# Expert products as plain 4-byte products in four column groups of 32, without splitting their operands

## The chip, the cores and the metric

The kernel runs on one core of a Trainium2 chip. The metric is the device time of one execution in microseconds. Before the change three runs gave a median of 1053.33 us (1052.43 to 1054.62).

## The reference

A two-branch encoder block over 512 tokens (and 16 learned ones ahead of them) with 1024 features, followed by a layer of 16 experts. What is changed lies in the experts. All tensors are 4-byte floats.

```python
h = layer_norm(DN_ALPHA * h + mixed, ln1_g, ln1_b)
ffn = moe_ffn(h, w_router, w_gate, w_up, w_down)
h = layer_norm(DN_ALPHA * h + ffn, ln2_g, ln2_b)
...
def moe_ffn(x, ...):
    # each token goes to the two best experts of its best group of four
    for e in range(N_EXPERTS):                       # 16
        h = silu(t @ w_gate[e]) * (t @ w_up[e])      # 1024 -> 512
        out = out + comb[:, e:e + 1] * (h @ w_down[e])   # 512 -> 1024
```

## The kernel before, in words

The span has three parts. Up to about 655 us the two branches of the mixer run; the change leaves them alone. From 655 to 729 us come the output projection, the first post-LN and the router. From 729 us on the 16 experts run, and behind them the second post-LN with the stores.

**The experts.** `order` (line 902) lets the four groups take turns, so that four experts in a row have no token in common. Each expert works only on its own tokens. Their places in a list of at most `CAP` = 112 come from the router (`idx`, one column for each expert), and their weights from `wsl`. For each expert:

- `gather` (line 1151) is an indirect DMA on GpSimd's queue that brings the tokens' rows from `h_dram` into `xg`.
- `xprep` (line 1159) transposes them by eight TensorE transposes with `ident` (L1164). ScalarE copies the result rounded (`xh`), VectorE subtracts for the rest (`xl`).
- `gu` (line 1168) makes the gate or the up product, 8 steps of 128 features into one PSUM tile `gu` of 128 places x 512 columns.
- `act` and `htr` (line 1195) multiply `silu(gate)` with up into `sg` and transpose it in four pieces (L1199), again split in `hh` and `hl`.
- `down` (line 1202) makes the down product into `py`, 4 steps of 128 x 2 halves of 512 columns.
- `add_rows` (line 1233) scales the rows by the tokens' weights on ScalarE and adds them to `o_dram` by one indirect DMA on GpSimd's queue, `scatter` (line 1155).

**The split.** No product takes 4-byte floats as they are. `split` and `unit` (line 1120) make from each megabyte of weights a rounded half `wh` (a cast on ScalarE, L233) and a lower half `wl` (a subtraction on VectorE, L236). One product then is three TensorE products, x-high with w-high, x-high with w-low, x-low with w-high. That gives 24 for gate, 24 for up and 24 for down, each 512 columns wide.

**Weights.** An expert has 6 MB, in six DMAs of 1 MB that SyncE issues (`fetch`, line 1109, which has the line 1114 in the waits). `slot` (line 1101) takes the next of 16 buffers in turn; SyncE waits until the split has read what was there.

**Order.** Every engine executes its instructions in the order in which a scheduler put them. In the loop at the end of the file the order of the program is: gate of expert i, `htr` of expert i-1, up of expert i, `xprep` of expert i+1, down of expert i-1. The scheduler interleaves them where operands come later. `overflow` counts experts that have more than `CAP` tokens; for the inputs here there is none, so that the loop for them at the end runs zero times. The first expert's tokens don't come by a gather. `place` (line 1043) picks them by products from the tiles `v` (`pso<-xg,v` in the profile). Line 91 is that of a helper that records instructions in program order; many rows have it.

The last expert runs beside the one before it and the second post-LN (`finish`, line 1288): its down product goes into two tiles `pye`, and the rows of `o_dram` are loaded back for the post-LN.

Of the kernel before, what the change touches and what calls it, by code (L numbers as in the profile page):

```python
# [22 lines left out]
S = 512  # L23
# [20 lines left out]
NX = 9  # L44
CAP = 112
# [3 lines left out]
RZ = 3  # L49
RMW = 240  # L50
FX = 1
H3, L3 = 1, 0
S3 = 2
S4 = 1
# [24 lines left out]
# the bits of the first guess of -1 / sqrt(2 x) are SEED less half those of x  # L79
# [3 lines left out]
class InOrder:  # L83
    """an engine whose instructions keep the order of the program"""
# [10 lines left out]
def hybrid_kernel(ctx, tc, x, meta_tokens, ln_in_g, ln_in_b, w_router, w_in, conv_w, conv_b,  # L95
# [27 lines left out]
    # ---------------------------------------------------------------- constants  # L123
# [31 lines left out]
    G.memset(epsc, EPS2)  # L155
    idx = consts.tile([128, NE], I32, name="idx")
    wsl = consts.tile([128, NE], F32, name="wsl")
    rest = consts.tile([128, NT], I32, name="rest")
# [57 lines left out]

    def halves(shape):
        """a pair for a split; while there is a third buffer it takes its turn"""
# [19 lines left out]
    # ---------------------------------------------------------------- phase 1  # L238
    with ExitStack() as p1:
# [14 lines left out]
        # as wide as the room between this pool and the next, so that the last scratch tiles make way for a slot  # L254
# [97 lines left out]
        # ---- head: input LayerNorm, transposes, split  # L352
# [52 lines left out]
        # mean and 1 / sqrt(var + eps) of two tiles and the meta tokens, then of the other two tiles  # L405
# [20 lines left out]
        # the weights of dt: four copies of the heads over the partitions  # L426
# [66 lines left out]
        # the residual in token layout waits in DRAM for the first post-LN  # L493
# [12 lines left out]
        # ---- dt and the cumulative decay  # L506
# [54 lines left out]
        # ---- pooling branch and gates  # L561
# [58 lines left out]
        # the router: scaled by the first post-LN, its column sums and its product with that LN's  # L620
        # shift, the latter two on every partition
# [13 lines left out]
        # ---- SSD: chunks of 128 tokens after one of the 16 meta tokens  # L635
# [120 lines left out]
        def g_out(g, wgt=None, ts=range(NT), ps2=()):  # L756
# [3 lines left out]
            for t, hf in [(t, hf) for t in ts for hf in range(2)]:  # L760
# [10 lines left out]
                if (t, hf) in POOLED.get(g, ()):  # L771
                    # the last groups' convolutions leave scratch tiles behind
# [136 lines left out]
        with tc.high_priority():  # L909
            G_ = InOrder(tc, G)  # L910
            for t in range(NT):
                (Q if t < QV else G_).dma_start(vt[t], h_dram[t * 128:(t + 1) * 128, :])
                if t == FX:
                    G_.dma_start(first, wu[order[0], 512:].rearrange("(k p) c -> p k c", p=128))
# [205 lines left out]
    def unit(r):  # L1120
        """a megabyte of expert weights, split in two"""
        ns[0] += 1
        if ns[0] <= 4:
            wh, wl = halves(r.shape)
            if ns[0] == 2:
                nsp[0] = 0
# [437 lines left out]
```

## Time and profile before

| | before |
|---|---|
| median of three runs | 1053.33 us |
| profiled execution, its span | 1047.7 us |
| TensorE (PE) busy in the span | 974.9 us |
| VectorE (DVE) busy | 805.0 us |
| ScalarE (ACT) busy | 520.1 us |
| GpSimd (POOL) busy | 189.1 us |
| first expert product starts at | 728.96 us |
| last product of the last `up` starts at | 1009.95 us |

The span is from the first to the last instruction of the profiled execution; the runs' time holds 5.6 us more. A row of the timeline has the start of the first instruction of a group in us from the span's start, the time until the end of the last, the engine, the line, the operation, the result and operands by name and shape, and the count. Consecutive instructions of one kind are drawn together. TensorE's ends are modelled, and its instructions overlap, so the distance from one start to the next tells what one costs. `PEld` is TensorE's loading of the stationary operand. In square brackets stands how long the engine was idle before, and what released it.

### The profile page before, as it was taken

The numbers are of one execution on the slowest core, as the hardware profiler recorded it, in microseconds if no ns is written. First come the engines' busy times: TensorE is split into PE (matmuls) and PEld (weight loads), VectorE is DVE, ScalarE is ACT, GpSimd is POOL, SyncE is SP. The second block draws the span as 40 slices with busy tenths as digits, with TensorE's granted clock in tenths as the row PEclk, the third lists the DMA queues.
The fourth block names the chain that finished last, engine by engine and source line by source line (L and its number), as shares of the span: only waits on it lengthen the run. The fifth ranks groups of instructions, "written<-read, shape, count | busy, mean of one in ns | idle before, by whom it ended". The sixth has DMA issues, their size and how long they took to land. (4 is left out here: it accounts for less than half of the span.)

```text
span 1047.7 us, 14476 instructions
## 1 busy us (share of the span) xinstructions
PE 974.9 (93%) x5664; PEld 842.5 (80%) x5664; DVE 805.0 (77%) x1225; ACT 520.1 (50%) x551; POOL 189.1 (18%) x129
## 2 busy tenths in 40 slices
PE   4989999999999999999999879989999999999970
PEld 3878888999898998989899767768788888888860
DVE  6887652476868686969797888398999999998973
ACT  4434333433525242525244352134778787888863
POOL 4930000000000000000000264144222222212134
PEclk9989999999999999999999998998999999999995
DMA  7442455423233232314232343975999999999854
GB/s 221 133 161 98 133 158 155 148 84 103 80 96 121 86 131 87 130 56 152 70 121 101 136 163 127 400 280 181 307 356 356 357 343 356 333 339 365 318 153 81
DMA packets 111350, 198.41 MB, mean 189 GB/s; under 512 B 7866, under 2 KB 54306, under 8 KB 110256
## 3 DMA queue, kind: packets, MB, share of 16 engines
q1 hardware_dynamic: 98320, 163.24, 45.6%
q0 software_dynamic: 6816, 18.09, 6.4%
q10 hardware_dynamic: 6144, 16.13, 4.2%
q8 instruction: 45, 0.74, 0.3%
q14 instruction: 25, 0.20, 0.1%
HBM read 186.05 MB, written 20.05 MB: 197 GB/s over the span
## 5 line engine op out<-in xcount | busy, mean ns | idle before, releaser
L236 DVE TENSOR_TENSOR wl<-raw,wh 128x2048 fp32r<-128x2048 f32 (+1 forms) x145 | 295.6, 2056 | 71.6 <-ACT wh L233 59.9
L233 ACT CAST wh<-raw 128x2048 fp32r<-128x2048 f32 (+1 forms) x145 | 242.8, 1696 | 164.3 <-PE ss L767 64.0
L1180 PE MATMUL gu<-wh,xhl 128*128 128x512 f32 x496 | 154.0, 394 | 0.1
L277 PE MATMUL mm<-hH,wh 128*128 128x264 f32 x624 | 129.1, 288 | 5.8 <-ACT ze L569 5.1
L277 PE MATMUL mm<-hH,wl 128*128 128x264 f32 x624 | 128.2, 287 | 0.0
L277 PE MATMUL mm<-hL,wh 128*128 128x264 f32 x624 | 127.7, 286 | 0.0
L776 POOL TENSOR_TENSOR acc<-acc,pre 128x512 f32<-128x512 f32 x12 | 19.2, 1621 | 529.2 <-ACT pre L775 529.2
L277 PEld LDWEIGHTS mm<-hH,wh 128*128 128x128 f32 x624 | 99.4, 190 | 9.1 <-ACT ze L569 5.3
L1180 PEld LDWEIGHTS gu<-wh,xhl 128*128 128x128 f32 x496 | 91.9, 188 | 18.3 <-DVE xhl L1166 0.5
L295 PE MATMUL mm<-hH,wh 128*128 128x512 f32 x256 | 102.5, 400 | 0.0
L295 PE MATMUL mm<-hL,wh 128*128 128x512 f32 x256 | 101.6, 397 | 0.0
L295 PE MATMUL mm<-hH,wl 128*128 128x512 f32 x256 | 101.5, 397 | 0.0
L277 PEld LDWEIGHTS mm<-hH,wl 128*128 128x128 f32 x624 | 98.4, 190 | 1.1
L277 PEld LDWEIGHTS mm<-hL,wh 128*128 128x128 f32 x624 | 97.7, 190 | 0.2
L1180 PE MATMUL gu<-wl,xhl 128*128 128x512 f32 x248 | 96.5, 394 | 0.0
L767 PE MATMUL ss<-wh,yy 128*128 128x512 f32 x192 | 67.4, 410 | 0.0
L1217 PE MATMUL py<-wh,hhl 128*128 128x512 f32 x224 | 67.0, 390 | 0.0
L295 PEld LDWEIGHTS mm<-hH,wl 128*128 128x128 f32 x256 | 48.2, 188 | 10.4
L295 PEld LDWEIGHTS mm<-hH,wh 128*128 128x128 f32 x256 | 48.2, 188 | 10.2
L295 PEld LDWEIGHTS mm<-hL,wh 128*128 128x128 f32 x256 | 48.1, 188 | 10.3
L1180 PEld LDWEIGHTS gu<-wl,xhl 128*128 128x128 f32 x248 | 46.5, 188 | 9.9
L1157 POOL DMA_INDIRECT o_dram<-hb,idx x13 | 26.0, 2000 | 153.4 <-ACT hb L1236 153.2
(373 smaller groups left out, 1752.9 us busy)
## 6 DMA issues: line engine op xcount, KB each, us to landing
raw<-in_w_exp_up_dram SPq DMA_DIRECT2D x29, 1024.0 KB, 14.4
raw<-in_w_exp_down_dram SPq DMA_DIRECT2D x29, 1024.0 KB, 14.8
raw<-in_w_in_dram SPq DMA_DIRECT2D x28, 1024.0 KB, 6.2
raw<-in_w_exp_gate_dram SPq DMA_DIRECT2D x28, 1024.0 KB, 17.0
M<-aD ACTq DMA_DIRECT2D x8, 1024.0 KB, 4.7
raw<-in_w_in_dram SPq DMA_DIRECT2D x16, 512.0 KB, 5.0
raw<-in_w_ssd_out_dram SPq DMA_DIRECT2D x8, 1024.0 KB, 4.9
ze<-eD ACTq DMA_DIRECT2D x16, 256.0 KB
```

The costliest lines, as they stand in the source:

```text
L233: A.copy(wh[:, c], src[:, c])
L236: (E[i] if E else V).tensor_sub(wl[:, c], src[:, c], wh[:, c])
L277: T.matmul(ps[:, i, :HF], lhsT=w[:, k, cs], rhs=h[k][:, i * HF:(i + 1) * HF], start=(n == 0), stop=(n == 3 * KT - 1))
L295: T.matmul(ps, lhsT=w[:, k, cs], rhs=h[k][:, NM:], start=(n == 0), stop=(n == 3 * KT - 1))
L767: T.matmul(ps, lhsT=y[:, j, t * 128:(t + 1) * 128], rhs=w[:, j, hf * 512:(hf + 1) * 512], start=(n == 0), stop=(n == 5))
L776: G.tensor_add(a, a, f)
L1157: return G.indirect_dma_start(out=dst, out_offset=off(ix), in_=src[:n], in_offset=None, **lim, **kw)
L1180: T.matmul(ps, lhsT=(xh, xh, xl)[n][:, u, k, :], rhs=us[u][n == 1][:, k, :], start=(i == 0), stop=(i == len(ms) - 1))
L1217: T.matmul(py[hf], lhsT=x_[:, 2 * u + k, :], rhs=ww[:, k, hf * 512:(hf + 1) * 512], start=(u == 0 and k == 0 and n == 0), stop=(u == 1 and ...
```

## The change

An expert's gate, up and down products take the 4-byte operands as they are, without a split. Only the last expert's down product stays as it was. A product has a stationary operand of 32 places instead of 128, and four such products, whose results go to different quarters of the PSUM partitions, are issued one after the other (`quad`). The room for places shrinks from 112 to 96 = 3 x 32. The first 64 places take half of the columns in each of the four groups: in a step of `gu` four products of 256 columns, two blocks of places by two halves. The last 32 places take a quarter of the columns in each: four products of 128. For `down` these are 512 and 256 columns.

The layout that comes out has consequences. `silu`, the multiplication and the copies are 384 wide instead of 512. `htr` has three transposes instead of four. A row of the result holds half of a token's columns or a quarter, so that `add_rows` adds by two scatters with tables of their own (`ixq`, `wq`, made by two small products at line 1103 from `sel`). Gate and up weights are fetched with pairs of neighbouring rows on a partition (`rows2`, 4 KB in one piece instead of 2), and the tokens are transposed with every second column (`cols2`). The buffers of the splits join the weight buffers, which are now 22.

```diff
-NX = 9
-CAP = 112
+NX = 10
+CAP = 96
+BK = 32
...
+    def rows2(E, r, src, r0):
+        n = r.shape[1] * 128
+        E.dma_start(r.rearrange("p (q j) c -> p q (j c)", j=2),
+                    src[r0:r0 + n, :].rearrange("(q p j) c -> p q (j c)", p=128, j=2))
...
-        us0 = [split(wg_[0], 4, copies=1)]
...
+        iws = small("iws", 2 * NE)
+        V.tensor_copy(iws, iw)
...
+        for i in range(2):
+            sel = xg1[:, 512 + 128 * i:640 + 128 * i]
+            T.matmul(pq[:, 2 * NE * i:2 * NE * (i + 1)], lhsT=sel, rhs=iws, start=True, stop=True)
...
-            A.copy(xh[:, i], p)
-            V.tensor_sub(xl[:, i], p, xh[:, i])
+            if i:
+                V.tensor_copy(xT[:, 4:, :n], p[:, :, :n])
+            else:
+                A.copy(xT[:, :4, :n], p[:, :, :n])
...
+    def quad(p, lhs, rhs, m, **kw):
+        for j in range(4):
+            T.matmul(p[BK * j:BK * (j + 1), m], lhsT=lhs(j), rhs=rhs(j), **kw)
...
     def gu(src, ws=None):
-        ms = [(u, k, n) for u in range(2) for k in range(4) for n in (0, 2, 1)]
-            T.matmul(ps, lhsT=(xh, xh, xl)[n][:, u, k, :], rhs=us[u][n == 1][:, k, :],
-                     start=(i == 0), stop=(i == len(ms) - 1))
+        for n in range(KT):
+            w, k = ws[n // 4], n % 4
+            quad(ps, lambda j: xT[:, n, BK * (j // 2):BK * (j // 2) + BK],
+                 lambda j: w[:, k, 256 * (j % 2):256 * (j % 2) + 256], slice(0, 256), start=(n == 0), stop=False)
+            quad(ps, lambda j: xT[:, n, 2 * BK:3 * BK], lambda j: w[:, k, 128 * j:128 * j + 128],
+                 slice(256, 384), start=False, stop=(n == KT - 1))
...
     def down(src, ws=None):
+        for n in range(4):
+            u, k = n // 2, n % 2
+            w = ws[u]
+            quad(p[:, 0], lambda j: hT[:, k, 2 * BK * (j // 2) + BK * u:2 * BK * (j // 2) + BK * u + BK],
+                 lambda j: w[:, k, 512 * (j % 2):512 * (j % 2) + 512], slice(0, 512), start=(n == 0), stop=(n == 3))
+            quad(p[:, 1], lambda j: hT[:, 2, BK * n:BK * n + BK], lambda j: w[:, k, 256 * j:256 * j + 256],
+                 slice(0, 256), start=(n == 0), stop=(n == 3))
...
-        A.activation(ys, py[2], AF.Copy, scale=w_)
-        sc = scatter(o_dram[:, :], fl(ys), ix, compute_op=OP.add).ins
+        for q, (c, n) in enumerate(((slice(0, 512), 2), (slice(512, 768), 4))):
+            A.activation(ys[:, c], p[:, q, :1024 // n], AF.Copy, scale=col_of(wq[q], i))
+            sc = scatter(o_dram[:, :].rearrange("s (h c) -> (s h) c", h=n), ys[:, c], col_of(ixq[q], i),
+                         compute_op=OP.add).ins
```

On TensorE, in the middle of the experts, the program before goes from the down products of one expert over both kinds of transposes to the up products of the next, and interleaves down and up. A row has the line, the operation, the result and operands, the result's partitions x columns and the waits; `wh` and `wl` are the halves of the weights, `xhl` and `hhl` those of the tokens.

```order
L1217 MATMUL py<-wl,hhl 128x512 x2
L1217 MATMUL py<-wh,hhl 128x512 x2
L1217 MATMUL py<-wh,hhl 128x512 [waits Activation_49]
L1199 MATMUL pt<-ident,sg 128x128 [waits DVE_49]
L1199 MATMUL pt<-ident,sg 128x128 x3
L1164 MATMUL pt<-ident,xg 128x128 [waits DMASW4_49]
L1164 MATMUL pt<-ident,xg 128x128 x3
L1180 MATMUL gu<-wh,xhl 128x512 [waits Activation_49]
L1180 MATMUL gu<-wh,xhl 128x512
L1217 MATMUL py<-wl,hhl 128x512 [waits DVE_49]
```

Each product there is a third of a step, and the transposes stand among them. The program after has at the same place, on TensorE, whole blocks; `raw` is a weight buffer as fetched, and `xT` and `hT` are the transposed tokens and hidden rows.

```order
L1181 MATMUL gu<-raw,xT 32x256 x4
L1181 MATMUL gu<-raw,xT 32x128 x4
L1172 MATMUL pt<-ident,xg_5731 128x96 [waits DMASW1_49,PE_49]
L1172 MATMUL pt<-ident,xg_5731 128x96 x3
L1172 MATMUL pt<-ident,xg_5731 128x96 [waits PE_49]
L1172 MATMUL pt<-ident,xg_5731 128x96 x3
L1181 MATMUL py<-raw,hT 32x512 [waits DMAHW5_49,Activation_49]
L1181 MATMUL py<-raw,hT 32x512 x3
L1181 MATMUL py<-raw,hT 32x256 x4
```

`xprep` now stands ahead of a whole `down`, and between quads; the three `htr` transposes stand in the same way between a gate and an up product. The waits for the lower halves are gone, and those for the fetches (DMAHW) stand at the products themselves.

At the start of the experts TensorE has, before, the first gate products behind the last small products of the router.

```order
L91 MATMUL ss<-to_6322,R 128x32 [waits DVE_49,Activation_49]
L91 MATMUL ss<-to_6329,R 128x32 [waits DVE_49,Activation_49]
L1180 MATMUL gu<-wh,xhl 128x512 [waits Activation_49]
L1180 MATMUL gu<-wh,xhl 128x512 x3
L1180 MATMUL gu<-wl,xhl 128x512 x4
```

After, the count for `overflow` (`py<-ohs,onesb`, which stood between the gate products) and the two products for the scatter tables stand between the router's last products and the first quad.

```order
L1447 LDWEIGHTS onesb
L1447 MATMUL py<-ohs,onesb 128x16
L1103 MATMUL ss<-iws,xg_5731 128x32 [waits DVE_49] x2
L1181 MATMUL gu<-rawh,xT 32x256 [waits DMAHW7_49]
L1181 MATMUL gu<-rawh,xT 32x256 x3
L1181 MATMUL gu<-rawh,xT 32x128 x4
```

The wait of the `ss<-iws` products is for VectorE's copy of the tokens' places and weights to `iws`, and the first quad stands behind it.

## Rows read from the trace of the kernel before

**Rows 1.** The page, section 1: busy us (share) and instructions of each engine.

```profile
PE 974.9 (93%) x5664; PEld 842.5 (80%) x5664; DVE 805.0 (77%) x1225; ACT 520.1 (50%) x551; POOL 189.1 (18%) x129
```

**Rows 2.** Windows: PE, PEld, DVE, ACT, POOL busy us (count), clock, DMA share, GB/s.

```profile
800.00:850.00 50.00, 50.00 (x239) 41.48 (x239) 45.57 (x32) 41.90 (x35) 13.23 (x6) 1.00 1.03 355
```

**Rows 3.** Waits of SyncE's queue from 700 to 1010 us: us in total, times, longest.

```profile
SPq L1114 <- DVE wl L236: 121.8, 46, 7.8
```

**Rows 4.** Timeline of PE around the start of the experts.

```profile
716.08 1.95 PE L91 MATMUL pso<-xg,v 128*128 128x128 f32 x16
...
728.59 0.53 PE L91 MATMUL ss<-to,R 128*128 128x32 f32 x4
728.96 1.17 PE L1180 MATMUL gu<-wh,xhl 128*128 128x512 f32 x4
...
737.36 1.06 PE L1164 MATMUL pt<-ident,xg 128*128 128x128 f32 x8 [2.46 <-DMA xg<-h_dram,idx]
```

**Rows 5.** Timeline of PE over one expert, from one group of htr transposes to the next.

```profile
759.37 0.60 PE L1199 MATMUL pt<-ident,sg 128*128 128x128 f32 x4
...
763.23 0.39 PE L1180 MATMUL gu<-wl,xhl 128*128 128x512 f32 x1
763.46 0.61 PE L1180 MATMUL gu<-wh,xhl 128*128 128x512 f32 x2
763.91 0.39 PE L1180 MATMUL gu<-wl,xhl 128*128 128x512 f32 x1
...
777.12 0.60 PE L1199 MATMUL pt<-ident,sg 128*128 128x128 f32 x4
777.56 0.60 PE L1164 MATMUL pt<-ident,xg 128*128 128x128 f32 x4
```

**Rows 6.** Timeline of the end: last up product, transposes, last down product, loads of o_dram.

```profile
1009.95 0.39 PE L91 MATMUL gu<-wl,xhl 128*128 128x512 f32 x1
...
1011.12 0.66 PE L91 MATMUL pt<-ident,sg 128*128 128x128 f32 x4 [0.78 <-DVE sg L91]
...
1012.45 0.73 PE L91 MATMUL pye<-wh,hhl 128*128 128x512 f32 x2 [0.68 <-ACT hhl L91]
1012.51 1.98 SPq L91 DMA_DIRECT2D raw<-o_dram  x4
```

**Rows 7.** Groups by form, PE, whole span: count, busy us, mean ns, idle before.

```profile
L722 PE MATMUL ss<-bc,XP 128*128 128x128 f32 x128 | 18.0, 281 | 0.0
L726 PE MATMUL ss<-M,XP 128*64 128x128 f32 x256 | 17.5, 279 | 0.0
...
L705 PE MATMUL ss<-Xd,Bk 128*128 128x256 f32 x32 | 9.3, 378 | 0.0
```

**Rows 8.** Timeline of PE in the mixer: whole-width products (L722) and two column groups (L726).

```profile
307.62 1.05 PE L722 MATMUL ss<-bc,XP 128*128 128x128 f32 x8
308.61 1.09 PE L726 MATMUL ss<-M,XP 128*64 128x128 f32 x16
309.63 1.16 PE L722 MATMUL ss<-bc,XP 128*128 128x128 f32 x8
310.72 1.09 PE L726 MATMUL ss<-M,XP 128*64 128x128 f32 x16
```

**Rows 9.** Timeline of PE: 256 columns (L705), 128x1 (L749) and small 2-byte products (L1388).

```profile
283.16 0.59 PE L705 MATMUL ss<-Xd,Bk 128*128 128x256 f32 x2
...
329.59 0.95 PE L749 MATMUL ss<-ones,ze 128*128 128x1 f32 x8
...
733.62 0.26 PE L1388 MATMUL py<-ohs,onesb 128*128 128x16 bf16 x4
```

**Rows 10.** Timeline of DVE in the router: pieces of a weight split.

```profile
708.17 2.50 DVE L236 TENSOR_TENSOR wl<-rawh,wh 128x512 fp32r<-128x512 f32 x4 [0.31 <-ACT wh L235]
```

**Rows 11.** Timeline of POOL in the experts: a scatter and a gather.

```profile
765.09 1.90 POOL L1157 DMA_INDIRECT o_dram<-hb,idx  x1 [10.78 <-ACT hb L1236]
767.30 2.52 POOL L1153 DMA_INDIRECT xg<-h_dram,idx  x1 [0.30 <-issue]
```

More of the change, by code (lines that the diff above doesn't have):

```diff
@@ new lines, in tile_of @@
+    def tile_of(pool, tag, **kw):
+        return lambda shape, dt: pool.tile(list(shape), dt, name="raw", tag=tag, **kw)
+    one, two = dict(bufs=1), dict(bufs=2)
+    places = ([tile_of(wsp, "wl3", **one)] + [tile_of(rawp, "raw")] * RP
+              + [tile_of(rawx[i], "raw") for i in range(RX - 2, -1, -1)]
+              + [hb_(1)] + [tile_of(ga, t) for t in ("ze", "XP", "yHL", "M")]
+              + [tile_of(wsp, t, **two) for t in ("wh", "wl")] * 2 + [tile_of(rawz, "raw")] * RZ
+              + [tile_of(hpool, "hL0"), tile_of(wsp, "wh3", **one), hb_(0), tile_of(rawx[RX - 1], "raw")])
@@ L1115, in fetch @@
             rs.append(r)
         return rs
-    ns = [1]
[L1120 to L1126, printed above, removed]
-            n = r.shape[1] // (0, 1, S3, S4)[ns[0] - 1]
-            for c in (slice(i, i + n) for i in range(0, r.shape[1], n)):
-                with tc.issue_after(exs[-1]):
-                    A.copy(wh[:, c], r[:, c])
-                with tc.issue_after(x_ins[-1]):
-                    V.tensor_sub(wl[:, c], r[:, c], wh[:, c])
-            return wh, wl
-        return split(r, 2 if ns[0] % 6 in SPL else 1)
@@ L1199, in htr @@
             T.transpose(p[:, k, :], h[:, k * 128:(k + 1) * 128], ident)
[L1200 to L1209 removed]
+        if n:
+            A.copy(hT[:, :n], p[:, :n])
@@ new lines, in htr_split @@
+    def htr_split(h, hhl):
+        MARK("htr")
+        p = psT.tile([128, 4, 128], F32, name="pt")
+        for k in range(3):
+            T.transpose(p[:, k, :], h[:, k * 128:(k + 1) * 128], ident)
+        for k in range(3):
+            if k == 2:
+                v = p[:, k, :].rearrange("p (a c) -> p a c", a=4)
+                h, l = (hhl[:, i, :, 2 * BK:] for i in range(2))
+            else:
+                v = p[:, k, :].rearrange("p (b u c) -> p u b c", b=2, u=2)
+                h, l = (hhl[:, i, k::2, :2 * BK].rearrange("p u (b c) -> p u b c", b=2) for i in range(2))
+            A.copy(h, v)
+            V.tensor_sub(l, v, h)
@@ new lines, in down @@
+    def down(src, ws=None):
+        MARK("down")
+        ws = ws or fetch(src, 256)
+        p = psY.tile([128, 2, 512], F32, name="py")
+        for n in range(4):
[5 more added lines that the diff above has]
+                 slice(0, 256), start=(n == 0), stop=(n == 3))
+        return p
@@ L1210, in down, with down_all, down_split @@
+    def down_all(src):
+        ws = fetch(src, 256)
+        p = psY.tile([128, 2, 512], F32, name="py")
+        for n in range(4):
+            for hf in range(2):
+                T.matmul(p[:, hf, :], lhsT=hT[:, n, :], rhs=ws[n // 2][:, n % 2, hf * 512:(hf + 1) * 512],
+                         start=(n == 0), stop=(n == 3))
+        return p
+    def down_split(us, hhl):
+        MARK("down")
+        py = [psG.tile([128, 512], F32, name="pye", tag="gu")[:CAP] for _ in range(2)]
         for u in range(2):
-            wh, wl = us[u] if us else unit(ws[u])
+            wh, wl = us[u]
```

228 lines of the change are left out of this document (105 added, 123 removed).

## The prediction

> **What bounds the kernel now.** I read the page first: TensorE (PE) is busy for 93% of the span [rows 1]. Then I read the span by windows. Between 800 and 850 us, deep in the experts, PE is busy for all 50 us at full clock. VectorE, busy with the splits, has 45.6 us and ScalarE 41.9, and the DMA engines show a share of 1.03 at 355 GB/s [rows 2]. So two things are full there, PE and the transfers. The waits say which ends last: SyncE, which issues the fetches, waits 121.8 us for the lower parts of the splits to free a buffer [rows 3], while PE waits for data only once, 2.46 us before the transposes at 737.36 [rows 4]. The experts run at the speed of PE. Work taken off VectorE and ScalarE there gives nothing by itself.
>
> One expert takes 777.12 - 759.37 = 17.75 us, from one group of `htr` transposes to the next [rows 5]. It holds 72 products of 512 columns: three from 763.23 to 763.91 take 0.68 us, 0.227 each. It also holds 12 transposes: four from 777.12 to 777.56, 0.11 each. 72 x 0.227 + 12 x 0.11 = 17.7, so nothing else stands on PE. From the first expert product at 728.96 to the end of the last at 1010.34 (1009.95 + 0.39) are 281.4 us [rows 4, 6].
>
> **Products.** A plain 4-byte product leaves two records: 64 products of L722 in the code have 128 records, 128 of L726 have 256 [rows 7]. Its record costs about 0.109 us for 128 columns (eight records of L722 in 1.05 us, of which 0.28 is the length of the last [rows 7, 8]) and 0.21 for 256 (two of L705 in 0.59, of which 0.378 is the second [rows 7, 9]); I take 0.215. So a column costs nearly four times what it cost in a split product, and only side-by-side work pays for that. The row for it is L726: two column groups of 64, sixteen records in 1.09 us, as long as eight records of L722 [rows 8]. Two groups cost what one costs. Four groups of 32 are in no row. I take them to overlap the same way, since L726 is the nearest row and loads as many stationary columns per record time (2 x 64 against 4 x 32).
>
> A step of `gu` is then 2 x 0.215 + 2 x 0.109 = 0.648 us, for 256 and 128 columns. 32 calls x 8 steps: 165.9 us. A step of `down` is 4 x 0.215 + 2 x 0.215 = 1.29 (512 columns taken as two of 256), 15 calls x 4 steps: 77.4. The sixteenth `down` keeps the split products and lies behind the stage in both kernels. Together 243.3. Accumulating products may run a little slower: sixteen records of L91 pso<-xg,v take 1.95 us, 0.112 each [rows 4], which would give 250. I take 245, near the lower end.
>
> **Transposes.** `htr` three instead of four, `xprep` eight of 96 places: 15 x (3 x 0.11 + 8 x 0.082) = 14.8 us, where 0.082 is 96/128 of 0.109, an estimate; at 0.109 it is 18.
>
> **Change of form.** Before, no expert work uses column groups. After, PE goes from quads to whole-width transposes and back twice for each expert (at `htr` and at `xprep`). From L722 to L722 at 309.63 with L726 between takes 2.01 us, from L726 to L726 at 310.72 takes 2.11; sixteen steps of 0.109 are 1.74 [rows 8]. A return trip costs 0.27 to 0.37 us; I take 0.35. 15 x 2 x 0.35 = 10.5; at 0.27 it is 8.1.
>
> **Waits on copies.** `xprep` now stands ahead of `down`, whose 5.2 us hide the two copies to `xT`; `htr` ahead of `up`, whose 5.2 us hide the copy to `hT`. Without that cover a copy costs what the end of before shows: transposes 1011.12, first product 1012.45, so 0.9 us behind the four transposes [rows 6]. That cover is missing at the last transposes ahead of the fifteenth `down` and partly at the first expert: 1.2 us.
>
> Sum of the stage: 245 + 14.8 + 10.5 + 1.2 = 271.5 against 281.4, **9.9 less**. Per expert that is some 17.3 against 17.75.
>
> **Start.** The tables of pieces need idx's counts copied and two products, which stand ahead of the first `gu`. In before `ss<-to,R` starts at 728.59 and `gu` at 728.96, with no wait [rows 4]; a copy on VectorE and two products put some 0.8 us there. Against it VectorE loses 2.50 us of splits at 708.17 in the router's chain [rows 10]. PE waits in that stage for other steps too, so between 0 and 2.5 us come back. I take nothing net. The 2.46 us wait is inside the 281.4 and goes, since `xprep` then stands behind two calls of `gu` (10.4 us) and not one.
>
> **Transfers.** Fetches now wait for PE instead of a split. Six more megabyte buffers let them start earlier and rows of 4 KB may run quicker than rows of 2 KB. No gain while PE binds.
>
> **GpSimd.** One scatter of 1.90 us becomes two, so 3.8; a gather of 2.52 beside them [rows 11] makes 6.3 us in 17.3. The gather is issued more than an expert ahead of its transposes. Nothing on the path, except at the end: the second scatter of the fifteenth expert holds back the loads of `o_dram`, issued at 1012.51 [rows 6], by about 2 us, partly beside the last products. I take 1.5 us lost.
>
> **Total.** -9.9 + 1.5 = -8.4 us. The profiled span is 1047.7; the median of the runs is 1053.33, so 5.6 lie around it, and unchanged. 1053.3 - 8.4 = **1045**.
>
> **Rivals.**
> 1. Groups don't fully overlap (0.08). Mechanism: the loads of a quad aren't hidden when all four groups change. Eight L749 products, each with a load of 128 columns and one column to multiply, need 0.95 us, some 0.11 each [rows 9], so 32 columns about 28 ns and four 0.11 us exposed on each quad; 40 quads an expert x 15.7 experts x 0.11 = 69 us: **1114**. Against it: L726 shows no such gap. The Trainium skill, "TensorE: Matmul & The Clock Gate", "Why this matters for your kernels", gives three column tiles of 32 with 512 columns as 2.38 times one, not three times. By that rule the products would take 245 / 0.79, an estimate, and the kernel 1110. L726 disagrees with it for two groups of 64, and no row here has more.
> 2. Only two groups run at a time (0.04): 245 us twice, **1290**. For it only that no row shows four.
> 3. The pairs of load and product come too slowly: this one ends slower (0.17). A quad of 128 columns has eight pairs in 0.218 us, 27 ns each. The densest row, four pairs of L1388 in 0.26 us of which 0.17 is the last's length, shows 25 to 30 ns [rows 9]. PE also has some 330 records an expert (2 x 160 and 11 transposes) where it had 84, so four times the instructions must be supplied. About 250 such quads have 2000 pairs, so each ns beyond 27 costs 2 us: from 31 ns on the gain is gone; 35 to 42 ns give **1061 to 1075**.
> 4. The transfers take PE's place (0.08). At 355 GB/s [rows 2] an expert's 6.29 MB need 17.7 us, no less than before. If 4 KB rows don't help, only the earlier start and the larger stock give something: **1051 to 1055**.
>
> **How the numbers follow.** Forecast 1036 to 1050: 0.63. Its lower end has cheap changes of form (-2.4), 2.5 back at the router, no loss at the end (-1.5) and 243 for the products; its upper end has 250 for them. The rivals have 0.17, 0.08, 0.08 and 0.04. About 0.2% is what a measurement here can tell from no change. Faster 0.63; within 0.2% 0.08 (rival 4); slower 0.29 (rivals 1 to 3). The range must leave out no more than 0.2: from 1036 to 1085 it leaves out rivals 1 and 2 and a little at each end. The forecast's own range is 1036 to 1050.
>
> **What would show it.** Starts of a 256-column quad's four records within some ns of each other and quads 0.43 and 0.22 us apart: overlap right. Experts 17.3 us apart by `htr`. About 0.15 and 0.2 us extra around each group of transposes. No wait of PE on DMA from 740 to 1000 us; if there is, rival 4. 128-column quads over 0.25 us: rival 3. Wrong altogether if the quads' records don't start together.

## The result, and where the time went

The changed kernel is slower. Its median is 1071.11 us (1068.69 to 1071.78, four runs) against 1052.88 (1051.03 to 1054.62, four runs): a ratio of 1.017, with a 95% interval of 1.0146 to 1.0194. The forecast was 1045, faster. The time lies inside the range, 1036 to 1085, and inside the 1061 to 1075 of rival 3, but that is luck: none of the rivals that stretched the range is the reason.

The profiled span is 1068.6 us against 1047.7. I cut both traces at two points, the start of the first expert product and the end of the last up product:

| | before | after | difference |
|---|---|---|---|
| from the start to the first `gu` | 728.96 | 747.62 | +18.7 |
| the stage: first `gu` to the end of the last | 281.4 | 277.7 | -3.7 |
| the end: from there to the last instruction | 37.4 | 43.3 | +5.9 |
| span | 1047.7 | 1068.6 | +20.9 |

So the part that the change was about did get shorter, and most of the loss lies in front of it, in a part whose arithmetic it hardly touches.

**The steady state.** Section 1 of the page after: busy us (share) and instructions of each engine. It answers [rows 1].

```profile
PE 988.0 (92%) x9580; PEld 803.0 (75%) x9580; DVE 575.9 (54%) x1088; ACT 333.2 (31%) x443; POOL 181.9 (17%) x154
```

Window of after, 50 us: busy us of PE, PEld, DVE, ACT and POOL (with counts), granted clock (1.00 is 2.4 GHz, 0.50 is 1.2), DMA share, GB/s. It answers [rows 2].

```profile
800.00:850.00 50.00, 50.00 (x961) 31.63 (x957) 3.34 (x6) 6.30 (x14) 12.36 (x9) 1.00 1.04 377
```

In these 50 us VectorE falls from 45.6 us to 3.3 [rows 2], the transfers go at 377 GB/s, and PE is still busy all the time at full clock. The waits of SyncE's queue from 700 to 1010 us (total, times, longest) answer [rows 3]: the wait for the lower halves is gone, and SyncE waits for PE, which is now the only thing that frees a buffer.

```profile
SPq L225 <- PE py L1181: 54.5, 21, 3.4
SPq L225 <- PE gu L1181: 50.5, 22, 4.0
```

Timeline of PE in after over one expert, the answer to [rows 5]: start, length, engine, line, operation, operands, shapes, count.

```profile
804.14 0.55 PE L1218 MATMUL pt<-ident,sg 128*128 128x128 f32 x3
804.62 5.41 PE L1181 MATMUL gu<-raw,xT 128*32 128x256 f32 x128
809.96 1.20 PE L1172 MATMUL pt<-ident,xg 96*128 96x96 f32 x8
811.09 5.37 PE L1181 MATMUL py<-raw,hT 128*32 128x512 f32 x64
816.27 5.38 PE L1181 MATMUL gu<-raw,xT 128*32 128x256 f32 x128
821.59 0.55 PE L1218 MATMUL pt<-ident,sg 128*128 128x128 f32 x3
```

From 804.14 to 821.59 are 17.45 us, where before had 17.75. A gate product takes 5.3 us for its 128 records. Each quad leaves two sets of four records. The starts of a set's four records lie 6 to 7 ns apart, and the next set follows after 0.216 us (256 columns) or 0.109 (128), so that quads are 0.43 and 0.22 us apart.

**The start.** Here is what GpSimd's queue holds around the loads of the residual `v`, first before, then after. `v<-h_dram` and the loads of `g1B` and `b1B` are DMAs that this queue issues.

```profile
653.95 1.32 POOL L91 DMA_DIRECT2D v<-h_dram  x2
...
662.40 1.05 POOL L91 DMA_DIRECT2D v<-h_dram  x2
```

```profile
674.18 0.47 POOL L924 IOTA xg<- 128x128 f32 x2 [19.70 <-PE pso L89]
674.75 1.33 POOL L89 DMA_DIRECT2D v<-h_dram  x2
...
676.77 0.56 POOL L89 DMA_DIRECT2D g1B<-in_ln_g_dram  x1
...
677.84 1.05 POOL L89 DMA_DIRECT2D v<-h_dram  x2
```

Two new instructions stand at the front: the IOTAs that begin the tables of pieces (`sel`, for the products at line 1103). They write into `xg1`, whose buffer TensorE is still reading for the output projection, so GpSimd waits 19.70 us. The loads behind them have nothing to do with that buffer, but they are in the same queue, and the first comes 20.8 us later than before (674.75 against 653.95), the last 15.4 (677.84 against 662.40). VectorE feels it first, in one row of its timeline in after (in before this instruction starts at 663.89):

```profile
682.63 0.69 DVE L951 SCALAR_TENSOR_TENSOR v<-v,ss 128x512 f32<-128x512 f32 x1 [7.66 <-DMA v<-h_dram]
```

and then PE. Its longest waits in after from 655 to 760 us, in total, times and longest (before has 0.8 for the same `pso` wait, and no other over 1.5 ahead of the first `gu`):

```profile
PE ss L89 <- DVE v L951: 5.0, 2, 3.4
PE pso L89 <- DVE v L951: 4.1, 1, 4.1
PE ss L89 <- DVE ohs L1014: 2.9, 1, 2.9
```

These are 12.0 us, but before waits in this part too. One window for each, from 655 us to its first `gu`, tells how much is new (before, then after; columns as above):

```profile
655.00:728.96 73.96, 66.00 (x366) 55.01 (x364) 51.96 (x191) 22.18 (x42) 24.02 (x21) 0.95 0.77 289
655.00:747.62 92.62, 78.95 (x375) 67.68 (x374) 52.49 (x201) 20.38 (x41) 24.68 (x23) 0.81 0.69 269
```

PE idles 13.7 us instead of 8.0, so 5.7 of the 18.7 are waits. The other 13 us are busy time: nine records more, and a granted clock of 0.81 instead of 0.95. This shows in the timeline of PE ahead of the first quad, the answer to [rows 4]:

```profile
724.82 0.66 PE L89 MATMUL ss<-ident,v 128*128 128x128 f32 x4 [3.40 <-DVE v L951]
725.31 3.35 PE L89 MATMUL pso<-xg,v 128*128 128x96 f32 x16
728.45 3.49 PE L89 MATMUL ss<-wrg,hT 128*128 128x16 f32 x16
731.78 3.71 PE L89 MATMUL pso<-xg,v 128*128 128x96 f32 x16
...
747.05 0.64 PE L1103 MATMUL ss<-iws,xg 128*128 128x32 f32 x2 [0.41 <-DVE wq L1106]
747.62 5.35 PE L1181 MATMUL gu<-rawh,xT 128*32 128x256 f32 x64
752.74 2.85 PE L1181 MATMUL gu<-raww,xT 128*32 128x256 f32 x64
```

After the wait of 3.40 us everything takes nearly twice its time. Sixteen records of `pso<-xg,v` need 3.71 us where before they needed 1.95 [rows 4], although they are narrower now (96 places, not 128). The first half of the first gate product takes 5.12 us (747.62 to 752.74) and the second 2.68. The windows say why. First before, then three of after, with the columns as above:

```profile
720.00:730.00 10.00, 7.67 (x67) 7.16 (x66) 8.63 (x41) 4.35 (x9) 3.49 (x3) 1.00 0.78 269
720.00:730.00 10.00, 6.60 (x36) 6.14 (x35) 8.03 (x30) 2.89 (x7) 5.43 (x5) 0.78 1.02 406
730.00:740.00 10.00, 9.45 (x48) 9.37 (x47) 3.89 (x28) 0.32 (x1) 1.80 (x2) 0.50 0.43 174
740.00:750.00 10.00, 8.85 (x67) 7.50 (x70) 6.42 (x37) 2.87 (x7) 1.96 (x2) 0.50 0.21 80
```

The granted clock is 0.50, the lower level, for 20 us in which PE is busy for 9.45 and 8.85 of 10. In before it is 1.00 from 720 to 750 us.

**The end.** Timeline of after around the end of the last up product, the answer to [rows 6]:

```profile
1023.06 4.50 DVE L89 TENSOR_TENSOR raw<-raw 128x2048 fp32r<-128x2048 f32 x2 [19.31 <-ACT raw L89]
...
1027.47 0.55 DVE L89 TENSOR_TENSOR sg<-sg,gu 128x384 f32<-128x384 f32 x1
...
1028.08 0.55 PE L89 MATMUL pt<-ident,sg 128*128 128x128 f32 x3 [2.75 <-DVE sg L89]
...
1030.22 8.50 PE L89 MATMUL pye<-raw 128*96 128x512 f32 x24 [1.60 <-ACT raw L89]
```

The last `down` keeps split products, and the split of its weights is the only one left. VectorE has been idle for 19.31 us and then does it exactly when `sg` becomes due: the up product ends at 1025.3, the multiplication starts at 1027.47. PE waits 2.75 us where before it waited 0.78 [rows 6], 1.60 us more for the halves of `hT`, and then the 24 products take 8.50 us, where before they took 5.8 (1012.45 to 1018.21).

### The profile page after: what moved, and what is told of

It is laid out like the page before. It is cut to its first block, busy times and chain, and to the rows that moved or that the text cites. A ratio compares the mean times of both kernels' runs of the same rounds, so it can differ in the third digit from the quotient of the medians.

```text
span 1068.6 us, 21961 instructions
## 1 busy us (share of the span) xinstructions
PE 988.0 (92%) x9580; PEld 803.0 (75%) x9580; DVE 575.9 (54%) x1088; ACT 333.2 (31%) x443; POOL 181.9 (17%) x154
## 3 DMA queue, kind: packets, MB, share of 16 engines
q1 hardware_dynamic: 82192, 163.24, 43.1%
## 4 chain that ended last, share of the span: by engine, by line
PE 79%; DMA 7%; DVE 6%; issue 5%; ACT 2%; POOL 1%; ACTq 0%; POOLq 0%; DVEq 0%
PE mm L293 21%; PE mm L311 16%; PE gu L1181 13%; PE ss L783 6%; PE py L1181 5%; PE pso L89 4%; DMA o_dram<-ys,ixq 4%; PE ss L89 1%; PE ss L738 1%; PE pt L1172 1%; PE ss L742 1%; PE mm L783 1%; PE ss L622 1%; DMA raw<-in_w_exp_up_dram 1%; DMA wdt<-in_w_in_dram 1%
## 5 line engine op out<-in xcount | busy, mean ns | idle before, releaser
L1181 PE MATMUL gu<-raw,xT 128*32 128x256 f32 (+1 forms) x3456 | 147.0, 326 | 1.5 <-issue 1.5
L252 DVE TENSOR_TENSOR wl<-raw,wh 128x2048 fp32r<-128x2048 f32 (+1 forms) x49 | 111.0, 2268 | 53.7 <-ACT wh L249 53.3
L1181 PEld LDWEIGHTS gu<-raw,xT 128*32 128x32 f32 x3456 | 105.9, 110 | 41.1 <-issue 3.7
L249 ACT CAST wh<-raw 128x2048 fp32r<-128x2048 f32 (+1 forms) x49 | 87.9, 1798 | 142.0 <-PE ss L783 64.0
L1211 DVE TENSOR_TENSOR sg<-sg,gu 128x384 f32<-128x384 f32 x15 | 8.3, 554 | 227.1 <-PE gu L1181 227.1
L1181 PE MATMUL py<-raw,hT 128*32 128x256 f32 (+1 forms) x832 | 70.0, 487 | 0.0
L1163 POOL DMA_INDIRECT o_dram<-ys,ixq x30 | 46.6, 1555 | 90.7 <-ACT ys L1292 77.8
L1181 PEld LDWEIGHTS py<-raw,hT 128*32 128x32 f32 x832 | 25.7, 110 | 39.0 <-issue 31.1
```

Of the source, the lines that this page charges most:

```text
L249: A.copy(wh[:, c], src[:, c])
L252: (E[i] if E else V).tensor_sub(wl[:, c], src[:, c], wh[:, c])
L1163: return G.indirect_dma_start(out=dst, out_offset=off(ix), in_=src[:n], in_offset=None, **lim(dst), **kw)
L1181: T.matmul(p[BK * j:BK * (j + 1), m], lhsT=lhs(j), rhs=rhs(j), **kw)
```

## The experiments

The theories after the comparison: **(A)** the IOTAs on GpSimd's queue cost the start; **(B)** narrower place products keep the clock at its lower level; **(C)** VectorE's subtractions cost the end; and against all of them **(R)** that the quads themselves, or the transfers they need, are the loss. (What the expectations of e6, e9 and e10 call theory C is B here.) "First `gu`", "stage" and "end" are the three parts of the profiled span, as above. Before was run beside each group; its medians were 1053.1, 1052.1 and 1053.0 (26 to 29 runs each). The ratio is the one on record and need not be the quotient of the medians. The three parts come from one profiled execution of each kernel.

| | median (range, runs) | ratio to before [95%] | first `gu` | stage | end |
|---|---|---|---|---|---|
| e1 | 1054.32 (1052.95–1060.16, 10) | 1.0029 [1.0007, 1.0052] | 734.12 | 275.6 | 42.8 |
| e2 | 1061.00 (1058.43–1066.25, 8) | 1.0079 [1.0056, 1.0103] | 738.43 | 281.6 | 37.4 |
| e3 | 1063.20 (1058.34–1068.05, 7) | 1.0096 [1.0066, 1.0126] | 734.30 | 283.9 | 40.0 |
| e4 | 1052.26 (1050.47–1058.26, 10) | 0.9974 [0.9937, 1.0010] | 733.78 | 274.3 | 43.1 |
| e5 | 1051.85 (1047.28–1053.42, 10) | 0.9986 [0.9965, 1.0007] | 734.37 | 273.1 | 37.8 |
| e6 | 1044.57 (1043.15–1047.08, 6) | 0.9924 [0.9895, 0.9952] | 731.30 | 271.7 | 38.3 |
| e8 | 1051.07 (1043.49–1052.97, 10) | 0.9964 [0.9938, 0.9991] | 736.35 | 272.1 | 40.0 |
| e9 | 1059.33 (1057.74–1064.46, 10) | 1.0076 [1.0054, 1.0098] | 741.45 | 272.9 | 41.6 |
| e10 | 1056.68 (1050.21–1060.77, 10) | 1.0003 [0.9960, 1.0046] | 733.26 | 288.1 | 37.0 |
| e11 | 1049.80 (1043.37–1053.19, 12) | 0.9934 [0.9895, 0.9973] | 731.91 | 271.9 | 38.9 |
| e12 | 1050.33 (1049.11–1055.74, 12) | 0.9958 [0.9924, 0.9992] | 731.18 | 274.0 | 43.3 |

**e1: the IOTAs behind the loads.** The changed kernel with the loop moved, nothing else.

```diff
-        for i, pat in enumerate(([[32, 2], [0, 2], [1, 32]], [[0, 4], [1, 32]])):
-            sel = xg1[:, 512 + 128 * i:640 + 128 * i]
-            G.iota(sel, pattern=pat, base=64 * i, channel_multiplier=0, **exact)
-            V.tensor_scalar(sel, sel, tokf[:, 0:1], None, op0=OP.is_equal)
...
                     G_.dma_start(b1B, bcast_row(ln1_b, D))
+        for i, pat in enumerate(([[32, 2], [0, 2], [1, 32]], [[0, 4], [1, 32]])):
+            sel = xg1[:, 512 + 128 * i:640 + 128 * i]
+            G.iota(sel, pattern=pat, base=64 * i, channel_multiplier=0, **exact)
+            V.tensor_scalar(sel, sel, tokf[:, 0:1], None, op0=OP.is_equal)
```

> The changed kernel with the two iotas for the scatter tables moved behind the loads of v on GpSimd's queue; nothing else is edited. Theory A: the iotas write a buffer that TensorE reads until 674 us, so GpSimd stands 19.7 us and the loads of v, g1B and b1B leave 20 us later; everything that is late at the first expert product (18.7 us: TensorE's waits of 4.1, 2.9 and 3.4 us and the lower clock behind each) follows from that. Then the first quad starts some 17 to 19 us earlier, near 729 to 731 us, and the time is 1071 - 18 = 1053, within 3 us. Rival B: the late loads cost only the wait at 684 us (3.3 us more than before), and the rest comes from what the missing splits do to the order of VectorE's work in the router and from the new work ahead of the first quad: then about 1067.

Measured: 16.8 us off the median, and the first `gu` comes 13.5 us earlier. The IOTAs run at the same time as in the changed kernel, since the buffer comes free when it did; only what is behind them on GpSimd's queue differs. POOL's timeline in e1, and one row of VectorE's:

```profile
654.04 1.34 POOL L89 DMA_DIRECT2D v<-h_dram  x2
...
662.52 1.05 POOL L89 DMA_DIRECT2D v<-h_dram  x2
673.74 0.47 POOL L935 IOTA xg<- 128x128 f32 x2 [10.16 <-PE pso L89]
...
674.04 0.48 DVE L936 TENSOR_SCALAR xg<-xg,tokf 128x128 f32<-128x128 f32 x2 [9.98 <-POOL xg L935]
```

VectorE, too, still waits 9.98 us for the IOTAs, ahead of the comparisons in the same loop (10.03 in after), so that this wait isn't the loss; the late loads are. A holds, and R can't explain it: no expert product was touched. It isn't the whole of the loss, though; the first `gu` is still 5.2 us later than before.

**e2: the same loop in the kernel before,** ahead of the loads; its result is not used there.

```diff
         xg1 = hpool.tile([128, D], F32, name="xg1", tag="hL2")
+        for i, pat in enumerate(([[32, 2], [0, 2], [1, 32]], [[0, 4], [1, 32]])):
...
```

> The kernel before with only these two iotas (and the two comparisons on VectorE that use them) put where the changed kernel has them, ahead of the loads of v; their result isn't used. Theory A: 1053 + 15 to 20 = 1068 to 1073 with the first expert product near 745. Rival B: 1056 to 1057.

Measured: 7.9 us slower than before, first `gu` 9.5 us later, stage and end unchanged to 0.3 us. GpSimd waits the same 19.70 us in its trace. So four lines whose result nobody reads cost 8 us. Theory A had 1068 to 1073 and its rival 1056 to 1057; 1061.00 is neither. It is half of what the loop's move gave in e1; e12 says where the other half is.

**e3: the last split earlier,** ahead of the last gate product (on top of e1).

```diff
+    for w, (wh, wl) in zip(wd_, us):
+        A.copy(wh, w)
+        V.tensor_sub(wl, w, wh)
     pg = gu(None, wg_)
...
-    for w, (wh, wl) in zip(wd_, us):
-        A.copy(wh, w)
-        V.tensor_sub(wl, w, wh)
```

> As e1, and the split of the last down weights moved ahead of the last gate product in the program. In the changed kernel VectorE subtracts these weights until 1027.5 us and so multiplies sg 2.2 us after the last up product is done; the last 24 products then run at the lower clock (8.5 us against 5.7 before). Theory: with the subtraction out of the way the multiplication starts with the last up product's end, the wait of 2.75 us at the transposes falls under 1 us, and the time is 2 to 5 us under that of e1. Rival: the end hangs on the two scatters and the loads of o_dram behind them (statistics at 1031), so that it stays within 1 us of e1.

A miss, for a reason of my own making. PE waits 0.75 us for `sg` instead of 2.75 and the 24 products take 5.78 us, so C holds at its place; but ScalarE's casts now stand in its queue ahead of a copy to `xT` and wait there for weights, and a gate product waits for that copy. Timeline of PE in e3:

```profile
981.89 7.17 PE L1181 MATMUL gu<-raw,xT 128*32 128x256 f32 x128 [6.38 <-ACT xT L1176]
```

It is the mistake of the IOTAs again, on another queue: the median rises by 8.9 us over e1.

**e4: one change of form for each expert.** `htr` stands next to `xprep` (on top of e1).

```diff
-        if i:
-            htr(hs.pop(i - 1))
         hs[i] = act(pg, gu(wu[e], None if i else wu_))
+        if i:
+            htr(hs.pop(i - 1))
         xprep
```

> As e1, with the htr transposes moved behind the up product, next to the xprep transposes, so that TensorE changes between quads and whole-width transposes twice instead of four times for each expert. If a return trip costs the 0.35 us read from the mixer, the time between two experts falls from 17.44 to 17.1 us and the whole by 14 x 0.35 = 5 us against e1. Rival: the copy of hT, which was hidden by the up product, is now hidden only by the eight xprep transposes (1.1 us for a copy of 0.5), and the gain is gone or turned into a loss of up to 0.5 us an expert.

Timeline of PE in e4:

```profile
817.15 10.77 PE L1181 MATMUL gu<-raw,xT 128*32 128x256 f32 x256
827.85 0.55 PE L1218 MATMUL pt<-ident,sg 128*128 128x128 f32 x3
828.23 1.09 PE L1172 MATMUL pt<-ident,xg 96*128 96x96 f32 x8
829.35 2.79 PE L1181 MATMUL py<-raw,hT 128*32 128x512 f32 x32
```

From one `htr` to the next are now 17.37 us on the mean against 17.45; the stage is 1.3 us shorter than in e1 and the median 2.1 lower, with overlapping ranges. The expectation was 5 us; the trip that went is worth less. By the starts of the records in after, the way from the last records of a gate product over three transposes to the first of the up product takes 0.68 to 0.70 us, where four plain steps of 0.109 give 0.44: a return trip costs some 0.25. At `xprep`, with steps of 0.120, it is 0.26 to 0.28. The joint trip in e4 costs some 0.3. So about 0.2 us were to be had for each expert, and 0.08 came on the mean. In seven of twelve experts all of it came: they are 17.19 to 17.24 us apart. The other five take 17.38 to 18.02; no row here shows what holds them up.

**e5: the last split between `silu` and the adding of rows** (on top of e4), behind the copies that others wait for.

```diff
     sg = silu(pg)
+    for w, (wh, wl) in zip(wd_, us):
+        A.copy(wh, w)
+        V.tensor_sub(wl, w, wh)
     for sc in add_rows(down(None, wp_), last - 1):
```

> As e4, with the split of the last down weights put between silu of the last gate product and the copies of the fifteenth down product, where ScalarE stood idle for 5.1 us and the weights had landed. Theory: the casts (3.7 us) fit into that gap and the subtractions end before the last up product, so that sg is multiplied at once; the wait at the last transposes falls from 2.75 to 0.75 us, the last 24 products run at 5.8 us and not 7.4 as in e3, and the time is 3 us under e4: 1049. Rival: the end hangs on the two scatters and the loads behind them: within 1 us of e4.

The end of e5, timeline of PE:

```profile
1008.15 0.55 PE L89 MATMUL pt<-ident,sg 128*128 128x128 f32 x3 [0.68 <-DVE sg L89]
...
1010.30 5.78 PE L89 MATMUL pye<-raw 128*96 128x512 f32 x24 [1.60 <-ACT raw L89]
```

In the profiles the end shrinks from 43.1 us (e4) to 37.8, nearly what before has, 37.4: 2.1 less waiting for `sg`, and 24 products in 5.78 us instead of 8.12. They are the same products. The wait for `sg` is as C says in all five traces with the split moved (e3, e5, e6, e8, e11: 0.68 to 0.75 us). The 24 products take 5.8 us in four of them, but 7.35 in e8, so the split alone doesn't settle their clock. The medians show 0.4 of the 3 us expected (1052.26 to 1051.85): the profiled execution of e5 is the fastest of its ten, which spread over 6 us. So C is shown as a wait in the trace, and what it is worth in the time is not.

**e6: place products 128 wide** (on top of e5), as in before. This computes columns that no one reads.

```diff
-                T.matmul(xps[k // 4][:, k % 4, :CAP], lhsT=cols2(vt[t], k), rhs=R0s[t][:, :CAP],
+                T.matmul(xps[k // 4][:, k % 4, :], lhsT=cols2(vt[t], k), rhs=R0s[t],
```

> As e5, with the products that place the first expert's tokens 128 columns wide again (as in the kernel before) instead of 96. In e1 the granted clock was 0.56 from 730 to 740 us, in the kernel before 1.00; before each both had a wait of 1.5 to 1.6 us. Theory C: the narrower products, which load as many stationary columns and stream fewer, keep TensorE at its lower level after the wait; at 128 the clock comes back during them and the first gate product, so that the first expert ends 3 to 5 us earlier: 1045. Rival: the lower level follows from the wait alone, the width does nothing: within 1 us of e5.

A third more columns in these products, and the kernel is 7.3 us faster at the median; all six runs lie below all ten of e5. The expectation was 1045. It is the fastest version, 0.9924 of before [0.9895, 0.9952], but on six runs of one chip. Two kernels built on it, with the same 128 columns, have medians near that of e5 (e8, e11 below), so the 7.3 us can't be relied on.

**e9: the changed kernel with the wide place products alone:** the edit of e6, nothing else.

> The changed kernel as it is, iotas ahead of the loads of v, with only the place products 128 columns wide. In the changed kernel the clock stayed at 0.50 from 730 to 750 us though TensorE was busy 9.45 of the first 10; in e2, with the same late loads and 128 columns, it came back at 728. Theory C (as in e6): the first quad some 4 to 8 us earlier than 747.6, and the time 1071 - 6 = 1065. Rival: the width does nothing, 1070 to 1072.

11.8 us off the median (6 were expected), with the IOTAs still in the way; the first `gu` is 6.2 us earlier, the stage 4.8 shorter. The wait at 724.99 is there as in after (3.37 us), and the group behind it is as slow, but the next isn't. Timeline of PE in e9:

```profile
725.49 3.31 PE L89 MATMUL pso<-xg,v 128*128 128x128 f32 x16
728.59 2.19 PE L89 MATMUL ss<-wrg,hT 128*128 128x16 f32 x16
730.63 2.13 PE L89 MATMUL pso<-xg,v 128*128 128x128 f32 x16
```

Windows of e9, columns as above:

```profile
730.00:740.00 10.00, 8.14 (x70) 7.70 (x70) 7.34 (x39) 1.70 (x6) 1.99 (x2) 1.00 0.57 228
740.00:750.00 10.00, 9.48 (x220) 7.08 (x224) 6.04 (x40) 1.95 (x3) 3.99 (x4) 1.00 0.51 148
```

Granted clock 1.00 twice, where after has 0.50 twice. PE executes the same instructions in the same order in both traces, apart from the width. So B holds for this kernel: the width made the clock come back behind the wait. It is not all that matters, as e8 shows.

**e10: the reverse in before,** the last three of the four groups of place products 96 wide.

```diff
-                T.matmul(xps[k // 4][:, k % 4, :], lhsT=vt[t][:, k * 128:(k + 1) * 128], rhs=R0s[t],
+                T.matmul(xps[k // 4][:, k % 4, :96 if t else 128], lhsT=vt[t][:, k * 128:(k + 1) * 128], rhs=R0s[t][:, :96 if t else 128],
```

> The kernel before with one edit: of the four groups of products that place the first expert's tokens, the last three are 96 columns wide instead of 128. Theory C: less is streamed for the same load of stationary columns, the clock stays at its lower level after the wait of 1.5 us at 723 us, and the first expert product comes 2 to 4 us later; the splits behind it then cover some of it: 1055 to 1057. Rival: the width alone does nothing here (columns that aren't streamed save time): 1053 within 1.

Inconclusive by its ratio (1.0003, 0.9960 to 1.0046). The median, 1056.68, is in the range of the theory, but no run is near it: five lie at 1050 to 1055 with a mean clock of 0.974 to 0.976, like most of before, and five at 1059 to 1061 with 0.966 to 0.969. The profiled execution took 1060.07:

```profile
729.00 3.70 PE L91 MATMUL pso<-xg,v 128*128 128x96 f32 x16 [0.55 <-DVE xg L1012]
```

```profile
730.00:740.00 10.00, 10.00 (x42) 8.55 (x42) 5.45 (x10) 3.10 (x5) 1.63 (x2) 0.65 0.60 185
```

The first fence is PE's timeline, the second a window: narrow products at the lower clock, and a clock of 0.65 in the first gate product, as in after. By the mean clocks of the runs, the narrow products seem to lose the clock in some executions of before and not in others; only one was profiled. Five of before's own 29 runs lie at 1064 to 1067 too, so width isn't the only way there.

**e12: both repairs of the start** (e1 and the wide place products) in the changed kernel.

> The changed kernel with the two repairs of its start alone: the iotas behind the loads of v (e1) and the place products 128 columns wide; the order of htr and the late split of the last down weights are left as they are. What the quads are worth when nothing at the start eats it: e1 was 1054.3; the first quad comes 3 us earlier and the first gate product runs 2.4 us faster, so 1048 to 1049, that is 4 to 5 us under the kernel before. Rival: the clock at the start varies from run to run for other reasons as well, 1052 to 1054.

20.8 us off the median: 1050.33, between the 1048 to 1049 expected and the rival's 1052 to 1054. On record it is 0.9958 of before [0.9924, 0.9992]; the two medians are 2.7 us apart. This, barely clear of noise, is what the change is worth with its start repaired. First `gu` 731.18, 2.2 us behind before; experts 17.45 us apart. The two repairs gave 16.8 and 11.8 alone, so they overlap by about 8. The late loads cost 16.8 us with narrow place products (after to e1) and 9.0 with wide ones (e9 to e12), near the 7.9 of e2. The narrow products cost 11.8 with late loads (after to e9) and 4.0 without (e1 to e12). (e1, e9 and e12 ran on three chips, on which before's medians differ by up to 1.1 us.) So part of what the late loads cost, they cost through the clock.

**e8: the scatter tables behind the first expert** (on top of e6), with their operands in buffers of their own, so that neither the copy to `iws` nor the products at line 1103 stand ahead of the first quad.

```diff
+    def tables():
+        ...
+            T.matmul(pq[:, 2 * NE * i:2 * NE * (i + 1)], lhsT=sels[i], rhs=iws, start=True, stop=True)
...
             with tc.high_priority(offset=-200):
+                tables()
                 overflow()
```

> As e6, with the two products for the scatter tables (and the copies that they wait for) behind the first expert's products instead of ahead of its first quad; their selection matrices lie in two constants that are no longer used by then. The first quad then waits only for the copies to xT. Expected: the first quad 1.5 to 2 us earlier than in e6 and the time as much lower, since the tables are wanted only by the first scatter, 17 us later. Rival: the first scatter or the gathers on GpSimd come late, and nothing is gained.

A miss: the first quad comes 5 us later than in e6. Two of ten runs were at 1043 and 1046, eight at 1050 to 1053. In the profiled execution PE waits 3.1 us for a VectorE step of the router that e6 has in another order. Timeline of PE in e8:

```profile
715.88 1.11 PE L89 MATMUL ss<-ident,v 128*128 128x128 f32 x4 [3.14 <-DVE v L952]
...
723.48 3.76 PE L89 MATMUL pso<-xg,v 128*128 128x128 f32 x16
```

The granted clock is 0.50 from 716 to 731 us, though the place products are 128 wide. So wide products alone don't bring the clock back; what does is open. What the tables themselves cost at the start isn't settled by this run.

**e11: transposes of 128 places** in `xprep` (on top of e6).

```diff
-                T.transpose(p[:, k, :n], cols2(xg[:n], 4 * i + k), ident[:n, :n])
+                T.transpose(p[:, k, :], cols2(xg, 4 * i + k), ident)
```

> As e6, with the xprep transposes of 128 places again (the last 32 are zeros and aren't copied). In the changed kernel a transpose of 96 places by 96 takes 0.120 us, not the 0.082 that I had worked out; the transposes of 128 take 0.109. Expected: 15 x 8 x 0.011 = 1.3 us less than e6, if the smaller form is what slows them. Rival: the place of its rows does it, no change.

No gain. Timeline of PE in e11:

```profile
824.23 1.12 PE L1172 MATMUL pt<-ident,xg 128*128 128x128 f32 x8
```

From start to start one costs 0.120 us at 128 places as at 96 in after. The median is 5 us above that of e6, though the two kernels differ in nothing else and the stage is as long (271.9 and 271.7): four of the twelve runs lie at 1043 to 1046, eight at 1049 to 1053. I take this as a warning on e6: more runs of it may spread as these do.

## Why the prediction was wrong

**What bounds the kernel, Products: right.** A step of `gu` was put at 0.648 us and takes 0.65 (5.32 for eight, with half a change of form in it); a step of `down` was put at 1.29 and takes 5.18 / 4 = 1.295. Four groups run as one. *Rival 1* (groups overlap only partly) falls with it. The figure quoted beside it from the Trainium skill, "TensorE: Matmul & The Clock Gate", "Why this matters for your kernels", is 2.38 times for three column groups. Carried over to four groups, as the prediction does, it would make a quad of 256 columns take 0.43 x 3 / 2.38 = 0.54 us, an estimate; the trace has 0.43, the time of one product. No run here has three groups. *Rival 2* needs quads of 256 columns 0.86 us apart and *rival 3* quads of 128 over 0.25; they are 0.43 and 0.22. *Rival 4* needs a wait of PE for transfers after 740 us; there is none that lasts.

**Transposes: mis-sized.** 0.082 for 96 places was scaled by width. They take 0.120, and so do 128 places (e11). 15 x 8 x 0.038 = 4.6 us more than the term. What differs from the 0.11 of before is that they read every second column; that this is the cause was not tried.

**Change of form: mis-sized the other way.** 0.25 to 0.28 us for a return trip instead of 0.35: 15 x 2 x 0.085 = some 2.6 us less. The lower end of the row range, 0.27, was the better guess.

**Sum of the stage: -9.9 became -3.7.** In steady state the two errors come to 0.1 to 0.2 us an expert (17.45 against "some 17.3"), 2 to 2.5 us. The other 4 us lie at the beginning of the stage and are not the quads': 64 records of the first gate product in 5.12 us instead of 2.6 at the lower clock (2.5 us), and a gap of 1.5 us at 773 us, in which PE waits for nothing that the profile shows. With the clock back, in e9, both are gone and the stage is 272.9 (-8.5); in e12 it is 274.0, in e6 271.7. The prediction gave the stage's length without asking in which clock it begins.

**Start: wrong, and this is what turned the sign.** "I take nothing net", with 0.8 us lost and up to 2.5 back; it was +18.7. Three things were missed there.
1. The step named the two products and the copy ahead of the first quad, but not the IOTAs that make their operand. They stand in GpSimd's queue ahead of the loads of `v`, and their target is a buffer that TensorE reads until 674 us. The paragraph **GpSimd** looked at scatters and gathers in the experts and concluded "nothing on the path"; the queue at 654 us was not looked at. e1 gives 13.5 us at the first `gu` and 16.8 in all; e2 gives 9.5 and 7.9 the other way, in a kernel with wide place products.
2. The narrower place products were not in the sum at all, as a saving of a few columns in a stage that isn't bound by them. They cost the clock: after to e9, 6.2 us at the first `gu` and 11.8 in all; e1 to e12, with the loads in time, 2.9 and 4.0. That wide products can run at the lower level too (e8) leaves open what the width does there.
3. The rest is 2.2 us (731.18 in e12 against 728.96). The step put 0.8 us at the products and the copy; in e12 the way from the router's last small products (`ss<-to,R`, 729.04) to the first quad takes 2.14 us where before has 0.37, so they cost 1.8. The 2.5 us that VectorE was to give back don't show.

**The end: mis-sized.** 1.5 us were taken, for the second scatter; 5.9 were lost. The scatter was the wrong place. VectorE, otherwise idle, does the last split just when `sg` is due, which costs PE 2.0 us, and the 24 last products run at a lower clock, 2.7 us longer than before. With the split moved the end is within 0.4 us of before in e5, both scatters included, and 0.9 to 2.6 us over it in e6, e11, e3 and e8.

**Total.** The prediction took 5.6 us around the span, the median less one span. Each run's own span is only 1.8 us shorter than its time (1068.6 and 1070.44 in after); by that, the profiled execution of before took 1049.5, 3.4 us less than its median. That is why the spans differ by 20.9 and the medians by 18.2.

The order listing in front of the prediction tells TensorE's side. The same listing of GpSimd's queue would have had two new instructions ahead of `v<-h_dram`, with a wait for TensorE.

## What to carry to other kernels

For each instruction that a change adds, however small, look at what its target buffer's last reader is and at what stands behind it on its queue: two IOTAs of 0.2 us cost 17 us by delaying loads that didn't need them, 9 of them even with wide place products. Judge the stage that leads into the tuned loop by its granted clock as well as by its work; cutting columns from products there cost 12 us in the changed kernel, more than the 8.4 that the whole change was to bring. And put the last remaining work of a kind (here one split) where its engine is idle, and behind, not ahead of, what others wait for.

## What the runs showed of the hardware that was not expected

- Four column groups of 32 with 4-byte operands start within 20 ns of each other and take the time of one product, 0.43 us for 256 columns and 0.22 for 128, at 1.00 of the clock with the transfers at 377 GB/s beside them.
- The place products take as long at 96 columns as at 128, at either level of the clock: sixteen records took 2.10 us (96, e1) and 2.13 (128, e9) at 1.00, and 3.71 (96, after) and 3.76 (128, e8) at 0.50. What differs is how long the lower level lasts. Behind a wait of PE of 3.4 us the clock was 0.50 for 20 us with 96 columns (after), with PE busy 92% of them, and with 128 it was back at 1.00 for the second group of place products (e9); behind one of 3.1 us it was 0.50 for 15 us with 128 columns too (e8). What decides that stays open.
- The change between column groups and whole width costs 0.25 to 0.28 us for a return trip. The Trainium skill, "TensorEngine Tiling (Array Packing)", "Key Properties", says that switching the mode drains TensorE. The trace shows a cost at each switch, and that is its size here; the drain itself stands in no row.
